# New prices in a planner of engine order, and a table that moves 312 groups of instructions, in a two-layer hybrid decoder

## The chip, the cores and the metric

The kernel runs on one core of a Trainium2 chip. The metric is the device time of one execution in microseconds (us). A core has five engines that run side by side, each through its own list of instructions: TensorE (PE in the profile; its weight loads are the row PEld), VectorE (DVE), ScalarE (ACT), GpSimd (POOL) and SyncE (SP), which here issues the loads and stores. They wait for each other by semaphores.

## The reference

The input is 1024 tokens of width 1024 in fp32, and there are two layers. A layer is a mixer and an FFN:

```python
for l in range(DEPTH):                          # 2
    h = rmsnorm(x, attn_norm[l])
    proj = h @ w_in[l]
    ...                                         # split into ten pieces
    y_a = mla_attention(...)                    # 4 heads, causal over all tokens, latent keys and values
    y_b = short_gated_conv(g_b, g_c, u_conv, conv_w[l])
    y_c = multiscale_pool(u_pool, pool_w[l], pool_scale[l])
    y_d = swa_sink_attention(...)               # 4 heads, window of 128 tokens
    ...                                         # each of the four normed over its 256 channels
    x = x + mixed @ w_o[l]
    h2 = rmsnorm(x, ffn_norm[l])
    gate, up = jnp.split(h2 @ w_gate_up[l], 2, axis=-1)
    x = x + (jax.nn.silu(gate) * up) @ w_down[l]
return rmsnorm(x, final_norm)
```

## The kernel before

**Layout and products.** Everything is held transposed: channels on the 128 partitions (rows), tokens along the free axis, in two halves of 512 tokens. fp32 products are made of three passes: an operand is split by ACT (the copy to `fp32r`, L281, L213 or L284) and by VectorE (what is left of it, L282, L214 or L285) into a high and a low part, and `mm3` (L270) multiplies high by high, high by low and low by high into one PSUM tile. PSUM tiles have four names with fixed buffers: `ps_mm` (2), `ps_s` (3), `ps_t` (2), `ps_pv` (1). Transposes (L479, L552, L942) and the sums over partitions for the norms (a product with a matrix of ones, L328) are true fp32; the rest of TensorE's work is `fp32r`.

**Stages.** Each layer goes through the input projection and the mixers, and then through the FFN, whose two matrix products are done with fewer block products (sums of weight blocks on GpSimd, L159, L1124 to L1126). In the mixer the steps that matter here are these. Sliding-window attention (`swa_unit`): scores L503, softmax, four transposes L552, split, products with the values L564, in 16 units per layer. Latent attention: values L270 into `ps_mm`, emptied by L820 and L821; for each of 4 heads and 2 halves, `scores` (L888 to L890), softmax, and `mix_values`: for each block of 128 keys transposes (L942) into a `ps_t` tile, the split into two tiles (L281, L282), and two products with the values (L954) into `ps_pv`. The output projection (L270 into `ps_mm`) is cut in parts and put between the heads. Its residual input is loaded at L1009, weights at L205, L210 and L257.

**What sets the order.** The program is first recorded in a written order. Then `order_engines` makes each engine's list anew. `steps_of` reads the instructions into steps (consecutive fp32 matmuls into one PSUM tile are one step) with their dependencies and a duration by kind. `arrange` plays the steps through a model of the five engines: at each point the engine that is free first takes, of its steps whose inputs are there and whose tiles have a free buffer, the one with the lowest rank, that is, the earliest in the written order. The sequence that comes out is fixed by dependencies between neighbours. The model's constants are matmul times (`MM_NS`), times between engines (`SIGNAL`), the overlap of neighbours on one engine (`OVERLAP`: VectorE's next instruction starts 82 ns before the end of the one before), and 92 ns on TensorE when an fp32 step follows an `fp32r` one. Nothing of this runs on the chip; only the lists do.

Of the kernel before, what the change touches and what calls it, by code (L numbers as in the profile page):

```python
# [1652 lines left out]
    "SP": {"PE": 50, "DVE": 35, "ACT": 35, "POOL": 80, "SP": 30},  # L1653
}
OVERLAP = {"DVE": 82, "ACT": 97, "POOL": 44}
FUNC_SETS = {"Silu": "Silu", "Exp": "Exp", "Ln": "Exp"}
ENGINES = {"PE": "PE", "DVE": "DVE", "Activation": "ACT", "Pool": "POOL", "SP": "SP"}


class Step:  # L1660
    __slots__ = ("ins", "eng", "rank", "before", "after", "tiles", "left", "ns", "tail", "ready", "sums", "bank", "onchip", "size", "start", "end", "table", "ls", "slotafter")

    def __init__(self, eng, rank):
        self.ins, self.eng, self.rank = [], eng, rank
        self.before, self.after, self.tiles = set(), [], set()
        self.ns = self.tail = self.ready = self.size = 0
        self.sums = self.bank = None
        self.onchip = False
        self.table = None


def areas(a):
# [25 lines left out]
DRAM_TILES = {"xs", "xp", "xr", "qd", "out"} | {f"ad{n}" for n in range(7)}  # L1698
# [34 lines left out]
def steps_of(tc):  # L1733
    steps, seen = [], {}
    table, runs = None, {"Silu": [], "Exp": []}
    for i in tc.nc.cur_bb.bb.instructions:
        kind = type(i).__name__
        if kind in ("BassTilePoolBoundary", "InstLoadActFuncSet"):
            continue
        eng = ENGINES[str(i.engine).split(".")[-1]]  # L1740
        ins = [a for a in i.ins if hasattr(a, "bass_ap")]
        outs = [a for a in i.outs if hasattr(a, "bass_ap")]
        fp32 = kind == "InstMatmult" and "float32r" not in str(i.ins[1].dtype)
        bank = outs[0].bass_ap.tensor.name
        v = steps[-1] if steps else None
        if not (fp32 and v and v.sums and v.bank == bank):
            v = Step(eng, len(steps))
            steps.append(v)
            v.bank, v.sums = bank, fp32
        v.ins.append(i)  # L1750
        if eng == "PE":
            n = width(outs[0])
            if fp32:
                one = i.ins[1].bass_ap.tensor.name.startswith("ones")
                v.ns += (867 if n == 512 else 534) if one else 108
                v.tail = 163 if one else 122
            else:
                v.ns = MM_NS[n]
                v.tail = 164 if n > 128 else 173
        elif kind == "InstDMACopy":  # L1760
            v.size = 4
            for s, n in outs[0].ap:
                v.size *= int(n)
            if eng == "POOL":
                v.ns, v.tail = 700, 4200
        else:
            v.ns = length(eng, kind, i, ins, outs)
            v.onchip = not any(a.bass_ap.tensor.name.startswith("ps_") for a in ins + outs)
            if eng == "ACT" and len(outs) > 1:
                v.tail = 61  # L1770
        f = FUNC_SETS.get(str(getattr(i, "func", "")).split(".")[-1])
        if f:
            other = runs["Exp" if f == "Silu" else "Silu"]
            if f != table:
                table = f
                runs[f] = []
            v.before |= set(other)
            runs[f].append(v)
            v.table = f
        for a, writes in [(a, False) for a in ins] + [(a, True) for a in outs]:  # L1780
            name, rects = areas(a)
            if kind == "InstCustomDveAnt":
                rects = [(0, 1 << 30, 0, 1 << 30)]
            if name.startswith("in_"):
                continue
            if name.split("_")[0] not in DRAM_TILES:
                v.tiles.add(name)
            seen.setdefault(name, [])
            for r, w, u in seen[name]:
                cross = name.startswith("ps_") and not (w or writes)  # L1790
                if cross or (w or writes) and any(
                    x[0] < y[1] and y[0] < x[1] and x[2] < y[3] and y[2] < x[3]
                    for x in r
                    for y in rects
                ):
                    v.before.add(u)
            seen[name].append((rects, writes, v))
    for v in steps:
        v.before.discard(v)
    return steps  # L1800


def arrange(steps, rank=lambda v: v.rank):
    queue, uses, freed, parked = {}, {}, {}, {}
    for v in steps:
# [3 lines left out]
        for name in v.tiles:  # L1809
            tag = name.rsplit("_", 1)[0]  # L1810
# [13 lines left out]
    now = {e: [] for e in SIGNAL}  # L1824
    out = {e: [] for e in SIGNAL}
    wire, pool_busy, last_fp32, table = 0.0, [], False, "Exp"
    for v in steps:
        if not v.left:
            heapq.heappush(later[v.eng], (0.0, rank(v), v.rank, v))
    while any(now.values()) or any(later.values()):  # L1830
        best = None
        for e in SIGNAL:
            if now[e]:
                t = free[e]
            elif later[e]:
                t = max(free[e], later[e][0][0])
            else:
                continue
            if best is None or t < best[0]:
                best = t, e  # L1840
        t, e = best
        while later[e] and later[e][0][0] <= t:
            _, k, n, v = heapq.heappop(later[e])
            heapq.heappush(now[e], (k, n, v))
        k, n, v = heapq.heappop(now[e])
        wait = None
        for name in v.tiles - live:
            tag = name.rsplit("_", 1)[0]
            if queue[tag][0] != name or not freed[tag]:
                parked[tag].append((k, n, v))  # L1850
                wait = -1
                break
            if freed[tag][0] + 40 > t:
                wait = max(wait or 0, freed[tag][0] + 40)
        if wait is not None:
            if wait > 0:
                heapq.heappush(later[e], (wait, k, n, v))
            continue
        for name in v.tiles - live:
            tag = name.rsplit("_", 1)[0]  # L1860
            live.add(name)
            queue[tag].popleft()
            heapq.heappop(freed[tag])
            for x in parked[tag]:
                heapq.heappush(later[x[2].eng], (t + 1, *x))
            parked[tag] = []
        v.start = t
        if v.size:
            if e == "SP":
                free[e] = t + 450  # L1870
                wire = max(t + 1400, wire) + v.size / 330.0
                v.end = wire + 600
            else:
                free[e] = t + v.ns
                v.end = t + v.ns + v.tail
        elif e == "PE":
            s = t + (92 if v.sums and not last_fp32 else 0)
            last_fp32 = v.sums
            free[e] = s + v.ns
            v.end = s + v.ns + v.tail  # L1880
        else:
            ns = v.ns
            if e == "DVE" and v.onchip:
                ns += 0.8 * sum(max(0.0, min(b, t + ns) - max(a, t)) for a, b in pool_busy[-8:])
            if v.table and v.table != table:
                table = v.table
                ns += 1280
            v.end = t + ns
            free[e] = v.end - OVERLAP[e]
            if e == "POOL":  # L1890
                pool_busy.append((t, v.end))
            if v.tail:
                free[e] = v.end - 10
                v.end += v.tail
        out[e].append(v)
        for name in v.tiles:
            todo[name] -= 1
            if not todo[name]:
                tag = name.rsplit("_", 1)[0]
                heapq.heappush(freed[tag], max(u.end for u in uses[name]))  # L1900
                for x in parked[tag]:
                    heapq.heappush(later[x[2].eng], (t + 1, *x))
                parked[tag] = []
        for w in v.after:
            x = free["PE"] if e == "PE" and w.eng == "PE" else v.end + SIGNAL["SP" if v.size else e][w.eng]
            if x > w.ready:
                w.ready = x
            w.left -= 1
            if not w.left:
                heapq.heappush(later[w.eng], (w.ready, rank(w), w.rank, w))  # L1910
    assert sum(map(len, out.values())) == len(steps)
    return out

def order_engines(tc):

    info = mybir.DependencyInfo(mybir.DependencyClass.NoSync, mybir.DependencyReason.DATA)
    for queue in arrange(steps_of(tc)).values():
        last = None
        for v in queue:
            for i in v.ins:  # L1920
# [131 lines left out]
```

## Time and profile before

| | us |
|---|---|
| median of 3 runs (lowest to highest) | 2083.02 (2080.73 to 2083.82) |
| profiled execution | 2081.12 |
| its span, first to last instruction | 2079.3 |
| TensorE busy | 2051.7 (99%) |
| VectorE busy | 1529.5 (74%) |
| ACT busy | 968.0 (47%) |
| GpSimd busy | 571.9 (28%) |

The span begins with the first layer's mixer (to about 416 us) and its FFN (to about 1092); the second layer's mixer runs to about 1456, its FFN to the end. How to read the rows that follow: in the rows by stretch, "a:b" is a stretch of the span, then its length, then the busy time and (instructions) of PE, PEld, DVE, ACT and POOL, the granted clock of TensorE as a share of full speed, the busy share of the DMA engines and GB/s. In rows in order of time, the first number is the start, the second the time from the first start to the last end of so many (x) instructions, and brackets hold the idle time of the engine before them with what ended it. In rows of the chain of work that ended last, the length of a piece is its share of that chain. A matmul is recorded from its start to the end of its results, while the next one starts earlier; so a busy TensorE need not be at its full pace.

### The profile page before, as it was taken

Reading aid. Unit: us, or ns where it says so; the run is one execution under the profiler, and the core shown is the slowest. Engines: PE = TensorE matmul, PEld = TensorE weight load, DVE = VectorE, ACT = ScalarE, POOL = GpSimd, SP = SyncE. Lnnn points to the kernel's source line nnn. Section 1 sums busy time; section 2 is a strip of 40 time slices with the busy share of each in tenths; the row PEclk is TensorE's granted clock in tenths of the full one; section 3 lists DMA queues with packets and bytes.
Section 4 is the critical chain, followed back from the end, with each engine's and each line's share of the span. In section 5 each row is a group of like instructions: output and inputs, shape, how many; then the busy total and the mean of one; then the engine's idle time right before and its main releaser. Section 6 shows DMA issues by size and latency. Waiting matters only on the chain.

```text
span 2079.3 us, 26320 instructions
## 1 busy us (share of the span) xinstructions
PE 2051.7 (99%) x9442; PEld 1679.6 (81%) x9442; DVE 1529.5 (74%) x2407; ACT 968.0 (47%) x1700; POOL 571.9 (28%) x453
## 2 busy tenths in 40 slices
PE   8999999999999999999999999999999999999997
PEld 6887777888888888888888877778888888888887
DVE  7878977977776777655657898869777677686555
ACT  6447656643333334444433566656433333354342
POOL 0000000037776775100000000000567677650000
PEclk9999999999999999999999999999999999999999
DMA  4110222424444446966401102232354444398652
GB/s 180 34 51 26 76 83 71 162 80 171 174 155 144 167 162 228 339 233 206 148 27 53 46 16 91 68 118 101 123 185 149 151 167 157 133 323 311 198 177 89
DMA packets 148819, 289.76 MB, mean 139 GB/s; under 512 B 12608, under 2 KB 72000, under 8 KB 148688
## 3 DMA queue, kind: packets, MB, share of 16 engines
q1 hardware_dynamic: 148656, 288.03, 40.1%
q8 instruction: 74, 1.21, 0.2%
q14 instruction: 57, 0.47, 0.1%
q0 software_dynamic: 32, 0.04, 0.0%
HBM read 204.66 MB, written 83.36 MB: 139 GB/s over the span
## 4 chain that ended last, share of the span: by engine, by line
PE 92%; DVE 6%; ACT 1%; DMA 1%; issue 0%; DVEq 0%; ACTq 0%; SPq 0%
PE ps_mm L270 34%; PE ps_s L270 29%; PE ps_t L270 12%; PE ps_pv L270 8%; PE ps_pv L954 2%; PE ps_t L942 1%; DVE u L282 1%; PE ps_s L888 1%; PE ps_pv L564 1%; PE ps_t L328 1%; PE ps_mm L762 1%; PE ps_s L503 1%; PE ps_s L890 1%; PE ps_s L889 1%; DVE u L340 1%; PE ps_t L552 1%
## 5 line engine op out<-in xcount | busy, mean ns | idle before, releaser
L270 PE MATMUL ps_mm<-u,u 128*128 128x512 f32 (+1 forms) x3376 | 825.8, 391 | 9.3 <-ACT u L284 7.1
L270 PEld LDWEIGHTS ps_mm<-u,u 128*128 128x128 f32 x3376 | 617.0, 189 | 131.6 <-ACT u L284 7.1
L270 PE MATMUL ps_s<-u,u 128*128 128x512 f32 x2672 | 630.7, 390 | 0.0
L270 PEld LDWEIGHTS ps_s<-u,u 128*128 128x128 f32 x2672 | 501.6, 188 | 106.3 <-issue 2.2
L282 DVE TENSOR_TENSOR u<-u,u 128x1024 fp32r<-128x1024 f32 (+2 forms) x368 | 443.4, 1230 | 148.7 <-ACT u L281 124.5
L281 ACT CAST u<-u 128x1024 fp32r<-128x1024 f32 (+2 forms) x368 | 321.1, 897 | 476.1 <-PE ps_mm L270 195.8
L270 PE MATMUL ps_t<-u,u 128*128 128x512 f32 (+1 forms) x1212 | 274.4, 379 | 0.0
L270 PEld LDWEIGHTS ps_t<-u,u 128*128 128x128 f32 x1212 | 219.1, 188 | 43.5 <-issue 1.4
L951 POOL MEMSET u<- 128x128 f32 x32 | 6.1, 217 | 865.8 <-PE ps_mm L270 628.8
L159 POOL TENSOR_TENSOR u<-u 128x256 f32<-128x256 f32 x176 | 188.4, 1071 | 68.9 <-DMA u<-in_w_dn 39.8
L1304 POOL TENSOR_TENSOR tp<-tp,u 128x512 f32<-128x512 f32 x88 | 144.0, 1638 | 223.2 <-ACT tp L1303 223.0
L270 PE MATMUL ps_pv<-u,u 128*128 128x512 f32 x696 | 164.9, 389 | 0.0
L270 PEld LDWEIGHTS ps_pv<-u,u 128*128 128x128 f32 x696 | 130.7, 188 | 27.1
L1303 ACT ACTIVATE tp<-tp 128x512 f32<-128x512 f32 x88 | 55.4, 632 | 119.6 <-DVE tp L340 118.6
L1124 POOL TENSOR_TENSOR u<-u,u 128x512 f32<-128x512 f32 x38 | 66.1, 1739 | 144.0 <-DMA u<-in_w_gu 81.9
L284 ACT ACTIVATE u<-u,par 128x512 fp32r<-128x512 f32 x100 | 69.9, 717 | 51.5 <-DVE u L1091 16.9
L282 DVE TENSOR_TENSOR u<-ps_t,u 128x512 fp32r<-128x512 f32 (+4 forms) x136 | 77.5, 584 | 21.7 <-ACT u L281 20.9
L281 ACT CAST u<-ps_t 128x512 fp32r<-128x512 f32 (+4 forms) x136 | 66.7, 505 | 57.0 <-PE ps_t L942 36.0
L285 DVE SCALAR_TENSOR_TENSOR u<-u,par,u 128x512 fp32r<-128x512 f32 x100 | 73.2, 751 | 8.3 <-ACT u L284 8.1
L1516 DVE TENSOR_TENSOR tp<-ps_mm,tn 128x512 f32<-128x512 f32 x38 | 26.3, 692 | 68.7 <-PE ps_mm L270 68.7
L214 DVE TENSOR_TENSOR u<-u,u 128x1024 fp32r<-128x1024 f32 (+1 forms) x46 | 51.8, 1129 | 33.2 <-ACT u L213 12.9
L1146 POOL TENSOR_TENSOR u<-u 128x512 f32<-128x512 f32 x38 | 68.3, 1797 | 8.9 <-DVE u L282 8.9
(186 smaller groups left out, 2240.2 us busy)
## 6 DMA issues: line engine op xcount, KB each, us to landing
u<-in_w_gu SPq DMA_DIRECT2D x88, 512.0 KB, 4.3
ad<-u SPq DMA_DIRECT2D x154, 256.0 KB, 2.5
u<-ad SPq DMA_DIRECT2D x70, 512.0 KB, 5.2
u<-in_w_dn SPq DMA_DIRECT2D x68, 512.0 KB, 3.9
qd<-u SPq DMA_DIRECT2D x44, 512.0 KB, 2.9
u<-qd SPq DMA_DIRECT2D x32, 512.0 KB, 4.7
u<-in_w_in SPq DMA_DIRECT2D x30, 512.0 KB, 3.5
u<-in_xT SPq DMA_DIRECT2D x32, 256.0 KB, 4.8
```

What stands on the lines that cost most here:

```text
L159: pool.tensor_tensor(out=o, in0=o, in1=u, op=ALU.add)
L214: dve.tensor_tensor(out=lo[:, :n], in0=raw[:, :n], in1=rd(hi[:, :n]), op=ALU.subtract)
L270: pe.matmul(o, w, r, start=start and k == 0 and i == 0, stop=stop and k == n - 1 and i == 2, skip_group_check=again,)
L281: act.copy(hi, f)
L282: dve.tensor_tensor(out=lo, in0=f, in1=rd(hi), op=ALU.subtract)
L284: act.activation(hi, f, AF.Copy, scale=gain)
L285: dve.scalar_tensor_tensor(out=lo, in0=f, scalar=gain, in1=rd(hi), op0=ALU.mult, op1=ALU.subtract)
L954: pe.matmul(py[:, c0:], v_of(j, h), R.ap(s)[:, c0:], start=j == 0 and n == 0, stop=j == nj - 1 and n == 1,)
L1124: pool.tensor_tensor(out=F.ap(q + 1), in0=a21, in1=a22, op=ALU.add)
L1146: pool.tensor_tensor(out=q4, in0=q4, in1=F.ap(self.raw[1] + 1), op=ALU.add)
L1303: last_silu = act.activation(g, g, AF.Silu)
L1304: pool.tensor_tensor(out=g, in0=g, in1=r, op=ALU.mult)
```

## The change

It touches the planner alone; what is computed stays. In `steps_of`, each step of an engine other than TensorE keeps the partition (row) at which its first input and its output start; two writes into one PSUM tile are now always ordered, as two reads were; the tiles of a step are a list in place of a set; and dependencies that follow from others are dropped. In `arrange`, VectorE and ACT start a step whose start rows differ from those of the one before only 31 and 24 ns after its end, in place of overlapping with it; after an fp32 step TensorE takes another ready fp32 step if there is one; a load of up to 128 KB is taken to land 1700 ns after its transfer in place of 600; steps parked for a buffer wake at a slightly later moment. And a table, `MOVES`, adds a number (from -300 to +164) to the rank of every step in 312 groups; a group is the steps of one engine on one output tile that stand near each other in the written order.

```diff
+SHIFT = {"DVE": 31, "ACT": 24, "POOL": 0}
...
+            if ins:
+                v.rows = tuple(areas(a)[1][0][0] for a in (ins[0], outs[0]))
...
-                cross = name.startswith("ps_") and not (w or writes)
+                cross = name.startswith("ps_") and w == writes
...
+    spare = [{u for w in v.before for u in w.before if u in v.before} for v in steps]
+    for v, far in zip(steps, spare):
+        v.before -= far
...
         k, n, v = heapq.heappop(now[e])
+        if e == "PE" and last_fp32 and not v.sums:
+            alike = [x for x in now[e] if x[2].sums and takes(x[2], t)]
+            if alike:
+                heapq.heappush(now[e], (k, n, v))
+                now[e].remove(min(alike))
+                k, n, v = min(alike)
+                heapq.heapify(now[e])
...
-                v.end = wire + 600
+                v.end = wire + (1700 if v.size <= 131072 else 600)
...
+            if v.rows:
+                rows, end = before[e]
+                if rows != v.rows and (rows[1] or v.rows[0]):
+                    t = max(t, end + SHIFT[e])
...
+MOVES = {
+    2: -39, 5: -32, 10: -33, 30: 2, 35: 5, 40: -8, 51: -20, 52: -31, 55: 88, 62: -146, 100: -12,
...
+    4598: 75,
+}
+
+
+def places(steps):
+
+    groups, last, at = {}, {}, {}
+    for v in steps:
+        k = v.bank, v.eng
+        if k not in groups or v.rank - last[k] > 60:
+            groups[k] = len(at)
+            at[groups[k]] = None
+        last[k] = v.rank
+        v.place = v.rank + MOVES.get(groups[k], 0)
+    return steps
...
-    for queue in arrange(steps_of(tc)).values():
+    for queue in arrange(places(steps_of(tc)), lambda v: v.place).values():
```

More of the change, by code (lines that the diff above doesn't have):

```diff
@@ L1660 @@
 class Step:
-    __slots__ = ("ins", "eng", "rank", "before", "after", "tiles", "left", "ns", "tail", "ready", "sums", "bank", "onchip", "size", "start", "end", "table", "ls", "slotafter")
+    __slots__ = ("ins", "eng", "rank", "before", "after", "tiles", "left", "ns", "tail", "ready", "sums", "bank", "onchip", "size", "start", "end", "table", "rows", "place")
     def __init__(self, eng, rank):
         self.ins, self.eng, self.rank = [], eng, rank
-        self.before, self.after, self.tiles = set(), [], set()
+        self.before, self.after, self.tiles = set(), [], []
         self.ns = self.tail = self.ready = self.size = 0
@@ L1668, in __init__ @@
         self.onchip = False
-        self.table = None
+        self.table = self.rows = None
 def areas(a):
@@ L1785, in steps_of @@
                 continue
-            if name.split("_")[0] not in DRAM_TILES:
-                v.tiles.add(name)
+            if name.split("_")[0] not in DRAM_TILES and name not in v.tiles:
+                v.tiles.append(name)
             seen.setdefault(name, [])
             for r, w, u in seen[name]:
-                cross = name.startswith("ps_") and not (w or writes)
+                cross = name.startswith("ps_") and w == writes
                 if cross or (w or writes) and any(
@@ L1826, in arrange @@
     wire, pool_busy, last_fp32, table = 0.0, [], False, "Exp"
+    before = {e: ((0, 0), 0.0) for e in SHIFT}
     for v in steps:
@@ L1829, in arrange, with takes @@
             heapq.heappush(later[v.eng], (0.0, rank(v), v.rank, v))
+    def takes(v, t):
+        for name in (x for x in v.tiles if x not in live):
+            tag = name.rsplit("_", 1)[0]
+            if queue[tag][0] != name or not freed[tag] or freed[tag][0] + 40 > t:
+                return False
+        return True
     while any(now.values()) or any(later.values()):
@@ L1845, in arrange @@
         k, n, v = heapq.heappop(now[e])
+        if e == "PE" and last_fp32 and not v.sums:
[5 more added lines that the diff above has]
+                heapq.heapify(now[e])
         wait = None
-        for name in v.tiles - live:
+        for name in (x for x in v.tiles if x not in live):
             tag = name.rsplit("_", 1)[0]
@@ L1858, in arrange @@
             continue
-        for name in v.tiles - live:
+        for name in [x for x in v.tiles if x not in live]:
             tag = name.rsplit("_", 1)[0]
@@ L1894, in arrange @@
                 v.end += v.tail
+            if v.rows:
+                before[e] = v.rows, v.end
         out[e].append(v)
@@ L1901, in arrange @@
                 for x in parked[tag]:
-                    heapq.heappush(later[x[2].eng], (t + 1, *x))
+                    heapq.heappush(later[x[2].eng], (v.start + 1, *x))
                 parked[tag] = []
```

34 rows, old and new, of the table MOVES are left out of this document.

## The prediction

> **What bounds the kernel now.** I read the page's first part, then the busy time by stretches, then the chain and the instructions in order of time at the places where TensorE loses time.
>
> ```profile
> span 2079.3 us, 26320 instructions
> PE 2051.7 (99%) x9442; PEld 1679.6 (81%) x9442; DVE 1529.5 (74%) x2407; ACT 968.0 (47%) x1700; POOL 571.9 (28%) x453
> ...
> 52.00:416.00 364.00, 359.68 (x1736) 286.94 (x1735) 308.20 (x700) 216.33 (x482) 3.02 (x16) 1.00 0.21 72
> 416.00:1092.00 676.00, 676.00 (x2994) 558.73 (x2993) 458.42 (x519) 267.72 (x379) 284.51 (x208) 1.00 0.50 172
> 1092.00:1456.00 364.00, 359.69 (x1719) 287.86 (x1718) 303.49 (x669) 213.27 (x462) 3.11 (x16) 1.00 0.21 70
> 1456.00:2028.00 572.00, 572.00 (x2523) 473.39 (x2523) 395.18 (x407) 222.82 (x299) 280.40 (x208) 1.00 0.54 189
> ```
>
> TensorE is the bound, and in the two FFN stretches (416 to 1092, 1456 to 2028) it is so without a gap. 572.00 us for 2523 matmuls are 226.7 ns each, the pace at which 512-wide products follow each other in the longest unbroken piece of the chain (22.44 us for 99):
>
> ```profile
> 828.22 22.44 PE ps_s L270 x99
> ...
> 2043.68 7.92 PE ps_mm L270 x66
> ...
> L270 PE MATMUL ps_s<-u,u 128*128 128x512 f32 x2672 | 630.7, 390 | 0.0
> L942 PE MATMUL ps_t<-cst,u 128*128 128x128 f32 x288 | 45.0, 275 | 1.0 <-DVE u L282 1.0
> L328 PE MATMUL ps_t<-u,ones 128*128 128x512 f32 x52 | 27.3, 613 | 0.8 <-DVE u L318 0.4
> ...
> 7.11 3.35 PE L270 MATMUL ps_mm<-u,u 128*128 128x512 f32 x6 [7.11 <-ACT u L284]
> ...
> 2069.35 0.70 PE L328 MATMUL ps_s<-u,ones 128*128 128x256 f32 x2 [1.48 <-DVE u L318]
> ```
>
> "99% busy" hides time lost in the other stretches, because a 512-wide product is recorded as 390 ns while the next starts after 227. So I count products instead, in the built program: 8148 of 512 columns (1846.9 us at 226.7 ns), 704 of 256 (84.5 at 120 ns, from 7.92/66), 80 of 384 (13.9, halfway between), 16 narrow ones (1), 424 transposes (45.8 at 108 ns, measured below), and 35 products with the ones, two passes of 613 - 163 = 450 ns (31.4; 163 is the overlap 390 - 227). Together 2023.5 us. From the first start, 7.11, to the last end, 2070.05 less that overlap, pass 2062.8. TensorE thus loses 39 us between its first and last product, 1.5 of it in the last wait (1.48 in the row); next to nothing of it is in the FFN, so some 37 lie in the start and the two mixer stretches (0 to 416, 1092 to 1456). Only 4.3 us in each of the two long mixer rows show as idle (364.00 less 359.68, less 359.69).
>
> The Trainium skill (Perfetto Trace Analysis, "Identifying the Most-Contended Engine") says that matmul busy time misleads, and to look at the weight loads' share. The trace agrees: 78.8% and 79.1% in the two mixer rows, against 82.7% and 82.8% in the FFN rows, under an equal 99 to 100% of matmul. By that measure the 574.8 us of loads in both mixer rows would need 695 us at the FFN's share, where they take 728: an estimate of 33 us lost, beside the 37 that my count gives with the start.
>
> **What the order of instructions shows.** In the built program the FFN stretches are the same instruction by instruction on TensorE; only the two mixers, their loads, and the last 30 us are reordered. So at most the 37 us and the last 1.5 us are at stake. The tail after the last product (2070.05 to 2079.3) keeps its chain; only its last stores swap places, all of one size: nothing.
>
> **Part 1, the gap at a change of partitions.**
>
> ```profile
> 58.36 0.69 DVE L428 TENSOR_TENSOR u<-te,u 64x512 fp32r<-64x512 f32 x1
> 59.08 0.69 DVE L431 TENSOR_TENSOR u<-te,u 64x512 fp32r<-64x512 f32 x1
> 59.80 0.69 DVE L340 TENSOR_TENSOR u<-ps_mm,u 128x512 f32<-128x512 f32 x1
> 60.41 0.35 DVE L513 CUSTOM_DVE_ANT_0 ps_s<-ps_s,cst,nsink 128x128 f32<-128x128 f32 x1
> ```
>
> L431 and L340 start 0.03 us after the end before them, L513 0.08 us before it: a change of the rows costs 0.11 us on VectorE. The program has 130 such changes before and 131 after: knowing them removes none. The direct worth is 0 (one more is 0.1 us on an engine that is 74% busy); the list merely stops planning on results that come 0.1 us later. The Trainium skill (VectorE: DVE Perf Modes, "Two Vector instructions with no wait between them") states it as hardware: an instruction whose operands start in another quadrant of partitions than those before it is held until all earlier ones have finished. The rows agree, and it speaks against any gain from this part alone: see the first rival.
>
> **Part 2, transposes taken together.** A new rule lets TensorE, after an fp32 step, take another ready fp32 step first. Changes from fp32r into fp32 fall from 147 to 110. Price, from this stretch of layer 1:
>
> ```profile
> 338.82 0.60 PE L942 MATMUL ps_t<-cst,u 128*128 128x128 f32 x4
> 339.17 0.48 PE L888 MATMUL ps_s<-u,u 128*128 128x512 f32 x1
> 339.49 0.39 PE L889 MATMUL ps_s<-u,u 128*128 128x512 f32 x1
> 339.72 0.40 PE L890 MATMUL ps_s<-u,u 128*128 128x512 f32 x1
> 339.95 0.60 PE L942 MATMUL ps_t<-cst,u 128*128 128x128 f32 x4
> 341.17 0.50 PE L954 MATMUL ps_pv<-u 128*128 128x512 f32 x1 [0.61 <-ACT u L281]
> 342.14 0.63 PE L942 MATMUL ps_t<-cst,u 128*128 128x128 f32 x4 [0.47 <-DVE u L282]
> 342.52 0.71 PE L954 MATMUL ps_pv<-u,u 128*128 128x512 f32 x2
> 343.12 0.66 PE L942 MATMUL ps_t<-cst,u 128*128 128x128 f32 x4
> 343.54 0.72 PE L954 MATMUL ps_pv<-u,u 128*128 128x512 f32 x2
> 344.49 5.27 PE L270 MATMUL ps_mm<-u,u 128*128 128x512 f32 x20 [0.24 <-ACT u L213]
> ```
>
> Four transposes last 0.60, the last of them 0.275 (its row's mean): 108 ns each. From 338.82 to 339.72 are 0.90 us for four of them (0.43) and two products (0.45): the change costs about 0.015. The kernel's own list prices it at 92 ns. So 37 changes are worth 0.5 us (3.4 by the list's constant). I take 0.5.
>
> **Part 3, the moved groups: three kinds of waits.**
> (a) The last head of a layer. From 339.95 to 344.49 TensorE does twelve transposes (1.30) and five products (1.13) in 4.54 us: 2.1 lost, since a transposed block needs ACT's copy and DVE's subtraction, 0.9 us from the last transpose (339.95 + 0.32) to the first product (341.17), and nothing else stands between. In the new order two blocks are transposed in a row, 0.85 us of scores follow, then four products together, later another pair of blocks with output-projection products between. Layer 2 adds a late weight:
>
> ```profile
> 1367.97 0.47 PE L954 MATMUL ps_pv<-u,u 128*128 128x512 f32 x1
> 1369.34 0.80 PE L270 MATMUL ps_mm<-u,u 128*128 128x512 f32 x2 [0.89 <-ACT u L213]
> ...
> 1362.81 5.57 DMA u<-in_w_o
> ```
>
> There the projection that waited 1.14 us (1.37 less one product) starts earlier in the new order. Of 2.1 and, for the like place with this, some 2.6 I take 3 as regained.
> (b) The value products.
>
> ```profile
> 233.49 0.40 PE L890 MATMUL ps_s<-u,u 128*128 128x512 f32 x1
> 235.09 0.70 PE L270 MATMUL ps_mm<-u,vhi 128*128 128x512 f32 x2 [1.21 <-DVE u L821]
> ```
>
> 1.60 less 0.23 is 1.37 lost until VectorE has emptied the bank. Between the last product into that bank and the next stand 1.5 us of work now, 2.4 in the new order, in both layers. Twice 0.85: 1.7.
> (c) All short covers. For each of the 96 split blocks of L942 I add up the TensorE work between its last transpose and its first product; under 1.2 us are 49 before, 34 after; of the 60 blocks of L552, 27 and 14. Together 76 and 48, 37% fewer; the medians go from 1.17 to 1.61 us and from 1.72 to 2.11. Of the 37 us, 4.7 + 2.7 are in (a) and (b), 2 in changes: 30 are left, of which I take a fifth, 6, as regained. The bounds are below nothing (the moves have opened new short covers, -2) and the full 37%, 11.
>
> Sum: 0 + 0.5 + 3 + 1.7 + 6 = 11.2, with the small start-up fillers some 12. The profiled execution took 2081.1 (span 2079.3 and 1.8 around it); the median of the runs is 2083.0. From it: 2071.
>
> **The rivals.**
> Full already, or not what it says: TensorE is 99% busy, the gaps stay (130 and 131) and the moves only shuffle. For it the page's row and the unchanged count; against it the 39 us counted and the longer covers. 2083. A twin, where the list's clock is off and the plan falls apart on the chip, gives 1 to 4 us: 2079 to 2082.
> Slower, by the load queue. SyncE issues all loads in one row, and a load that stands earlier but waits for its place holds those behind it:
>
> ```profile
> SPq L205 <- PE ps_pv L564: 67.0, 6, 35.0
> ```
>
> The longest such wait is 35.0 us already. The new order moves weight and residual loads in both mixers. If a weight tile then lands late by one load (5.57 us in the row above), TensorE loses up to 4; it takes four such tiles to eat the 12 us and pass the mark: 2087 to 2091. Against it: the idle times of TensorE quoted above name work of ACT or DVE; only the 0.89 goes back to a load.
> Larger: the places are so well chosen that two thirds of the 37 us go: 2059 to 2063.
>
> **How the numbers follow.** Forecast, 2064 to 2077: 0.62. Larger gain, below 2064: 0.12. A small gain, 2077 to 2082: 0.13, most of it beyond 0.2% (4.2 us, about what a measurement of this kernel can tell from no change). Full already: 0.07. Slower: 0.06. So faster 0.84, within 0.2% 0.10, slower 0.06. The range 2060 to 2080 reaches into the larger and the small gain and leaves out about 2 in 10.
>
> **What would show it.** TensorE's busy time near 2042 with the same 9442 instructions; weight-load share of the mixer stretches above 80%; the waits of 0.61, 0.47 and 1.21 us gone or halved; the FFN stretches at 226.7 ns. A mixer stretch as long as before, or waits of TensorE for loads, would prove it wrong.

## The result and the profile after

The changed kernel takes 2068.16 us (median of 4 runs, 2066.81 to 2069.08); the kernel before, in the runs beside it, 2082.47 (4 runs, 2080.73 to 2083.82). The ratio is 0.9931, 95% interval [0.9914, 0.9948]: 14.3 us faster. From one profiled execution to the other, 2081.12 to 2069.08, it is 12.0. The forecast was 2071 in a range of 2060 to 2080.

The first part of the page of the changed kernel, and its busy time by stretches (columns as before: length, then PE, PEld, DVE, ACT, POOL, clock, DMA share, GB/s):

```profile
span 2067.3 us, 26298 instructions
PE 2043.4 (99%) x9442; PEld 1681.0 (81%) x9442; DVE 1533.3 (74%) x2407; ACT 966.2 (47%) x1700; POOL 568.9 (28%) x453
```
```profile
52.00:416.00 364.00, 362.35 (x1763) 294.14 (x1762) 311.85 (x704) 217.69 (x483) 2.83 (x16) 1.00 0.21 72
416.00:1092.00 676.00, 674.20 (x2983) 556.40 (x2981) 451.21 (x511) 266.61 (x377) 280.79 (x208) 1.00 0.50 173
1092.00:1456.00 364.00, 362.08 (x1749) 293.83 (x1748) 308.83 (x673) 217.30 (x467) 6.60 (x19) 1.00 0.21 72
1456.00:2028.00 572.00, 571.54 (x2537) 473.18 (x2536) 400.28 (x412) 220.21 (x300) 277.75 (x206) 1.00 0.54 187
```

The same 9442 matmuls now take 2043.4 us of TensorE. In both mixer rows the share of weight loads rose, from 78.8% and 79.1% to 80.8% and 80.7%: more products got through in the same 364 us. But the first FFN row, full before (676.00 of 676.00), now has 1.8 us of idle time and a smaller weight-load share, 82.3% instead of 82.7%. The windows stand still while the work moves forward through them, so I also count the loss directly. **Loss** below is, summed over a stretch, the time from the start of one TensorE instruction to the start of the next, less the pace of its kind (226.7 ns for a 512-wide product, 108 for a transpose, and so on as in the prediction).

| loss, us | mixers and start (0 to 416, 1092 to 1456) | FFNs | all, with the last wait |
|---|---|---|---|
| before | 38.7 | 0.7 | 40.9 |
| after | 23.4 | 3.9 | 28.9 |

So the mixers gave 15.3 us, and the FFNs took 3.2 back. The two sites that the prediction named, in the order of time of the changed kernel's TensorE:

```profile
228.47 0.39 PE L890 MATMUL ps_s<-u,u 128*128 128x512 f32 x1
229.12 0.36 PE L270 MATMUL ps_mm<-vhi,u 128*128 128x256 f32 x1 [0.27 <-DVE u L821]
...
335.85 1.03 PE L942 MATMUL ps_t<-cst,u 128*128 128x128 f32 x8
337.46 0.73 PE L270 MATMUL ps_mm<-u,u 128*128 128x512 f32 x2 [0.57 <-ACT u L213]
338.03 0.39 PE L954 MATMUL ps_pv<-u 128*128 128x512 f32 x1
...
1252.32 0.40 PE L890 MATMUL ps_s<-u,u 128*128 128x512 f32 x1
1252.91 0.70 PE L270 MATMUL ps_mm<-u,vhi 128*128 128x512 f32 x2 [0.19 <-DVE u L821]
...
1356.07 1.03 PE L942 MATMUL ps_t<-cst,u 128*128 128x128 f32 x8
1358.49 3.85 PE L270 MATMUL ps_mm<-u,u 128*128 128x512 f32 x15 [1.39 <-ACT u L213]
```

The value products, which waited 1.21 us for VectorE, wait 0.27 and 0.19. At the last head of layer 1 eight transposes now run in one piece, and the idle time of 0.61 and 0.47 us for ACT and VectorE is gone. In its place stands a wait for ACT's copy of a weight (L213). Such waits are not new, only longer: before, those for L213 at the last heads were 0.24 us in layer 1 and 0.89 in layer 2. The chain shows what that copy waited for:

```profile
330.72 5.84 DMA u<-in_w_o
336.57 0.84 ACT u L213
...
1351.52 0.19 PE ps_pv L954
1351.71 0.02 SPq L205
...
1351.76 5.77 DMA u<-in_w_o
```

A weight of the output projection arrives late in both layers, 5.84 and 5.77 us after its issue. That is the late weight tile of the prediction's "slower" rival, at 0.57 and 1.39 us instead of up to 4. That another load held it back, as the rival has it, does not show here: in layer 2 its issue (L205) follows the end of a product (L954).

### The profile page after: what moved, and what is told of

Its sections match the earlier page's. It is cut to its first block, busy times and chain, and to the rows that moved or that the text cites. A ratio compares the mean times of both kernels' runs of the same rounds, so it can differ in the third digit from the quotient of the medians.

```text
span 2067.3 us, 26298 instructions
## 1 busy us (share of the span) xinstructions
PE 2043.4 (99%) x9442; PEld 1681.0 (81%) x9442; DVE 1533.3 (74%) x2407; ACT 966.2 (47%) x1700; POOL 568.9 (28%) x453
## 3 DMA queue, kind: packets, MB, share of 16 engines
q8 instruction: 74, 1.21, 0.2%
## 4 chain that ended last, share of the span: by engine, by line
PE 95%; DVE 2%; DMA 1%; ACT 1%; POOL 1%; issue 1%; DVEq 0%; SPq 0%; ACTq 0%
PE ps_mm L270 36%; PE ps_s L270 29%; PE ps_t L270 12%; PE ps_pv L270 7%; PE ps_pv L954 2%; PE ps_t L942 1%; PE ps_t L328 1%; PE ps_s L888 1%; PE ps_pv L564 1%; PE ps_s L890 1%; PE ps_s L889 1%; PE ps_s L503 1%; PE ps_t L552 1%; DMA u<-in_w_o 1%; PE ps_mm L762 1%
## 5 line engine op out<-in xcount | busy, mean ns | idle before, releaser
L270 PE MATMUL ps_mm<-u,u 128*128 128x512 f32 (+1 forms) x3376 | 836.8, 390 | 9.1 <-ACT u L284 7.1
L270 PE MATMUL ps_s<-u,u 128*128 128x512 f32 x2672 | 639.0, 390 | 0.7 <-ACT tn L1168 0.7
L270 PE MATMUL ps_t<-u,u 128*128 128x512 f32 (+1 forms) x1212 | 292.1, 380 | 0.0
L159 POOL TENSOR_TENSOR u<-u 128x256 f32<-128x256 f32 x176 | 188.1, 1069 | 69.9 <-DVE u L282 31.8
L270 PE MATMUL ps_pv<-u,u 128*128 128x512 f32 x696 | 170.6, 389 | 1.5 <-ACT tn L1168 1.1
L1303 ACT ACTIVATE tp<-tp 128x512 f32<-128x512 f32 x88 | 55.2, 632 | 121.4 <-DVE tp L340 120.6
L340 DVE TENSOR_TENSOR tp<-tp,u 128x512 f32<-128x512 f32 x76 | 67.6, 889 | 1.1
L316 ACT ACTIVATE tn<-u 128x512 f32<-128x512 f32 (+1 forms) x93 | 52.9, 589 | 32.8 <-DVE u L1569 28.3
```

The costliest lines, as they stand in the source:

```text
L159: pool.tensor_tensor(out=o, in0=o, in1=u, op=ALU.add)
L270: pe.matmul(o, w, r, start=start and k == 0 and i == 0, stop=stop and k == n - 1 and i == 2, skip_group_check=again,)
L316: act.activation(q, f, AF.Square)
L340: dve.tensor_tensor(out=o, in0=a, in1=b, op=ALU.mult)
L1303: last_silu = act.activation(g, g, AF.Silu)
```

## Experiments

The theories: (A) the moved places bring the gain and the rules are nearly free; (B) the rules, by telling the planner the truth, bring it; (C) neither does much alone, since the table was made for this planner. Unless a diff says otherwise, each kernel is the changed kernel with the one edit shown, so the small edits to how steps are read (ordered writes, the list of tiles, the later wake) stay in all of them. The kernel before, on the same chips, ran at 2082.49 us (first four kernels: the two halves, first_layer_moves, pool_kept), 2081.32 (the next four) and 2081.22 (the last three).

### The two halves: rules_alone and table_alone

```diff
-        v.place = v.rank + MOVES.get(groups[k], 0)
+        v.place = v.rank
```

> The table is emptied; the new prices and rules of the planner stay. Changes into fp32 on TensorE: 128 (147 before, 110 with the table). Theory A (the moved places bring the gain): 2078 to 2082 us, a gain of 1 to 4, and most waits in both mixers stay. Theory B (the list's better clock brings it, since it no longer plans on results that come late): 2070 to 2074 us.

```diff
-        if e == "PE" and last_fp32 and not v.sums:
+        if False and e == "PE" and last_fp32 and not v.sums:
...
-                v.end = wire + (1700 if v.size <= 131072 else 600)
+                v.end = wire + 600
...
-                if rows != v.rows and (rows[1] or v.rows[0]):
+                if False and rows != v.rows and (rows[1] or v.rows[0]):
```

> The table stays; the gap at a change of rows, the rule of taking fp32 steps together and the 1700 ns for small loads are taken back. Changes into fp32: 126. Theory A: 2069 to 2075 us. Theory B: 2078 us or more, since the places were chosen for another clock. A third, that the two need each other: both this and the rules alone gain under 5 us, and the sum falls short of the 14 of both.

The rules alone take 2077.50 us (ratio 0.9975 [0.9965, 0.9985]), the table alone 2078.76 (0.9982 [0.9973, 0.9992]): 5.0 and 3.7 us, 8.7 if they added, where both together give 14.3. So C, though neither half is idle: some 4 to 6 us come only where table and rules meet. It is 5.6 between the medians, with intervals of some 2 us or more on each term, and 4.0 by the loss of the mixers in the profiles (38.7 before, 32.9 and 33.2 with one half, 23.4 with both). The table's own entries in the FFNs show too: with the rules alone the FFNs lose 0.9 us, with the table alone 4.0.

### One layer's moves: first_layer_moves

```diff
-        v.place = v.rank + MOVES.get(groups[k], 0)
+        v.place = v.rank + (MOVES.get(groups[k], 0) if groups[k] < 2000 else 0)
```

> Only the table's entries up to group 1279 (the first layer) stay, with all rules. If the gains are local and add up: the first mixer is as short as in the changed kernel, the second as with the rules alone, and the time lies about halfway, 2073 to 2076. If a layer's order hangs on the other's: outside of that.

2073.10 us (0.9952 [0.9937, 0.9967]). The loss of layer 1's mixer with the start is 13.6 us, as in the changed kernel (13.4); layer 2's is 15.5, near that of the rules alone (14.1), where the changed kernel has 10.0; a stretch of halved clock, told of below under part 3 (c), is 1.7 of the 15.5. The moves work where they stand; one layer's do not need the other's.

### The FFN waits: pool_kept, no_ffn_moves, pool_price

In the changed kernel TensorE takes the products of the FFN in another order and stands still there. First its order of time before, where a tile gets its 24 products in one piece:

```profile
460.84 5.60 PE L270 MATMUL ps_t<-u,u 128*128 128x512 f32 x24
```

Then the changed kernel, its order of time, ACT's and the waits:

```profile
463.44 0.39 PE L270 MATMUL ps_t<-u,u 128*128 128x512 f32 x1
463.66 0.39 PE L270 MATMUL ps_s<-u,u 128*128 128x512 f32 x1
...
467.94 3.04 PE L270 MATMUL ps_s<-u,u 128*128 128x512 f32 x12 [0.72 <-ACT tn L1168]
...
503.14 2.88 PE L270 MATMUL ps_pv<-u,u 128*128 128x512 f32 x12
505.86 2.88 PE L270 MATMUL ps_mm<-u,u 128*128 128x512 f32 x12
509.82 3.01 PE L270 MATMUL ps_pv<-u,u 128*128 128x512 f32 x12 [1.08 <-ACT tn L1168]
512.68 0.61 PE L270 MATMUL ps_mm<-u,u 128*128 128x512 f32 x2
```
```profile
507.72 0.63 ACT L1303 ACTIVATE tp<-tp 128x512 f32<-128x512 f32 x1 [6.51 <-DVE tp L340]
508.26 1.03 ACT L281 CAST u<-u 128x1024 fp32r<-128x1024 f32 x1
509.19 0.58 ACT L1168 COPY tn<-ps_pv 128x512 f32<-128x512 f32 x1
```
```profile
PE ps_pv L270 <- ACT tn L1168: 1.1, 1, 1.1
PE ps_s L270 <- ACT tn L1168: 0.7, 1, 0.7
```

The twelve products of 503.14 fill the one `ps_pv` buffer. ACT should empty it at 506.02, but its copy (L1168) stands in ACT's list behind L1303, which waits 6.51 us for a VectorE result, and behind a cast. ACT is busy 39% of that row and still late: an in-order list holds a ready copy behind one that is not ready. TensorE is held the same way. The Trainium skill (TensorE: Matmul & The Clock Gate, "The mechanism") says that matmuls start and end strictly in their order. The trace is in line with it: the `ps_mm` products of 512.68 came behind the ones that waited 1.08 us; whether they were ready sooner, it does not show.

First suspect was GpSimd, whose FFN list had changed too. pool_kept chains its instructions in the order of before; TensorE's list stays that of the changed kernel:

```diff
+    for row in POOL_ROWS:
+        for a, b in zip(row, row[1:]):
+            steps[b].before.add(steps[a])
```

> The changed kernel, with GpSimd's list in both FFN stretches held in the order that it had before (TensorE's list is the same as in the changed kernel). If the new waits of TensorE in the FFN (1.1, 0.7 and 0.5 us for ACT's copies) come from GpSimd's swapped steps: they go, and the time falls by 2 to 3.5 us, to 2065 to 2066. If they come from the earlier arrival at the FFN with loads or stores not further on: they stay, 2068.

2069.71 us (0.9939 [0.9924, 0.9954]): no help, and the waits for L1168 stay, 1.9 and 1.6 us. The second suspect was the six entries of the table that fall in the FFNs, all on TensorE: `ps_t` and `ps_s` products of layer 1, `ps_mm`, `ps_s`, `ps_t` and `ps_s` of layer 2, 12 to 48 products each.

```diff
-    1106: -110, 1111: -40, 1112: -44, 1116: -37, 1140: -41, 1146: 57, 1263: -6, 1279: -31, 2267:
+    1106: -110, 1111: -40, 1112: -44, 1116: -37, 1140: -41, 1146: 57,   2267:
...
-    163, 3463: -25, 3581: 22, 3586: 22, 3620: -51, 4570: 95, 4583: 119, 4589: 83, 4595: 134,
+    163,     4570: 95, 4583: 119, 4589: 83, 4595: 134,
```

> The changed kernel without the table's six entries that lie in the FFN (groups 1263, 1279, 3463, 3581, 3586 and 3620); both mixers keep all moves. If these six make the new waits of TensorE in the FFN (2.8 us in layer 1, 1.0 in layer 2 of the changed kernel): the waits go, 2064 to 2066 us. If the waits come from something else (an earlier arrival, GpSimd's chain): 2067 to 2069, with the waits in place.

2064.57 us (4 runs, 2064.22 to 2064.94; 0.9921 [0.9906, 0.9936]), faster than the changed kernel by 3.6 between medians, and by 2.4 if each is set against the kernel before beside it (16.8 gained, and 14.3). TensorE's order differs from the changed kernel's only where the six entries stand, in stretches of 117, 36 and 149 instructions. The time by stretches and the same place in the order of time:

```profile
416.00:1092.00 676.00, 676.00 (x3001) 559.08 (x2999) 456.40 (x514) 267.13 (x378) 282.06 (x208) 1.00 0.50 173
...
1456.00:2028.00 572.00, 572.00 (x2559) 474.83 (x2558) 395.06 (x415) 220.89 (x301) 267.95 (x202) 1.00 0.54 187
```
```profile
502.27 2.88 PE L270 MATMUL ps_pv<-u,u 128*128 128x512 f32 x12
504.99 2.88 PE L270 MATMUL ps_mm<-u,u 128*128 128x512 f32 x12
507.71 2.88 PE L270 MATMUL ps_pv<-u,u 128*128 128x512 f32 x12
```

Both FFNs are full again, their loss falls from 3.9 to 0.5 us, and no wait for L1168 is left. Here ACT's L1303 starts at 504.65, in time. The six entries were the cause. pool_price asks instead whether the planner's low price of a 256-wide GpSimd addition is to blame (760 ns, where the trace of after has 1069 for L159):

```diff
-        return 206 if kind == "InstMemset" else 230 + 2.07 * n
+        return 206 if kind == "InstMemset" else 1150 if n == 256 else 230 + 2.07 * n
```

> The changed kernel, with GpSimd's 256-wide sums priced at 1150 ns in the planner, as the profile has them (1071 ns mean), and not at 760. TensorE's list is the same as in the changed kernel. If the new FFN waits come from plans that hold GpSimd free too early: they shrink, 2064 to 2067 us. If they come from TensorE's own order: 2067 to 2069.

2067.22 us (2066.57 to 2068.31; 0.9934 [0.9919, 0.9949]). Its runs overlap those of the changed kernel, so no gain is shown; TensorE's list is the same. Measured beside no_ffn_moves, it is the fair partner for the six entries: 2.7 us, with no overlap of the runs.

### The rules beside the table: no_grouping, no_gaps, price_15

```diff
-        if e == "PE" and last_fp32 and not v.sums:
+        if False and e == "PE" and last_fp32 and not v.sums:
```

> The changed kernel without the rule that takes ready fp32 steps together. Changes into fp32: 121 in place of 110. By the price of 15 ns that the trace of before gives: 0.2 us for the changes themselves. If only the changes count: 2068 to 2069 us. If the rule is part of the plan that the table was made for (the moves need the same rules): 2070 to 2075, with longer waits at other places. By the list's 92 ns the changes alone would be 1.0 us.

```diff
-                if rows != v.rows and (rows[1] or v.rows[0]):
+                if False and rows != v.rows and (rows[1] or v.rows[0]):
```

> The changed kernel without the gap at a change of rows in the planner; the table stays. The prediction gave this part a direct worth of 0. If it only serves the plan, as the need of table and rules for each other says: 2071 to 2077 us, since 130 starts on VectorE come 0.11 us later than planned and the moves were made for the right times. If it is worth nothing: 2067 to 2069.

2075.33 us (0.9972 [0.9961, 0.9982]) and 2076.37 (0.9978 [0.9968, 0.9987]): leaving out either rule costs 7.2 and 8.2 us between medians, and 8.3 and 9.4 if each is set against the kernel before beside it, though the first changes the number of changes into fp32 by only 11 (121 for 110), 0.2 us at 18 ns each. One can explain that in two ways: the rule is right and the plan needs a true clock, or any other planner spoils the table. The third kernel helps to tell these apart. It makes one price *truer*:

```diff
-            s = t + (92 if v.sums and not last_fp32 else 0)
+            s = t + (15 if v.sums and not last_fp32 else 0)
```

> The changed kernel with the planner's price of a change into fp32 at 15 ns in place of 92, the size that both traces show; 114 changes in place of 110, 49 short covers in place of 48. If a truer clock makes a better list: 2068 or less. If the table holds only for the planner as it stands, wrong price included: slower, 2070 to 2076.

2075.46 us (7 runs, 2074.84 to 2076.56; 0.9971 [0.996, 0.9983]): 7.3 slower than the changed kernel (8.6 if each is set against the kernel before beside it). A truer price costs as much as a missing rule. Waits of TensorE that are not among the changed kernel's stand in the profile of each (no_gaps, no_grouping, price_15, in this order):

```profile
PE ps_mm L270 <- DVE te L340: 1.4, 1, 1.4
PE ps_s L888 <- ACT u L281: 1.1, 1, 1.1
PE ps_s L888 <- ACT u L907: 1.0, 1, 1.0
```
```profile
PE ps_s L888 <- ACT u L281: 1.1, 1, 1.1
...
PE ps_s L888 <- ACT u L907: 1.0, 1, 1.0
```
```profile
PE ps_s L888 <- ACT u L281: 2.2, 2, 1.1
PE ps_mm L270 <- DVE te L340: 1.9, 2, 1.6
...
PE ps_s L888 <- ACT u L907: 1.4, 2, 1.0
```

The first scores of the attention (L888) wait for ACT in all three. So what a rule is worth beside this table is not the time that it describes: with any of the three changed, the list is no longer the one for which the places fit. That the truer price costs time because of the table, and would not without it, was not run.

### The places themselves: shifted_moves

```diff
+NEXT = dict(zip(MOVES, [*MOVES.values()][1:] + [*MOVES.values()][:1]))
...
-        v.place = v.rank + MOVES.get(groups[k], 0)
+        v.place = v.rank + NEXT.get(groups[k], 0)
```

> The changed kernel with each number of the table given to the next group of the table: the same 312 groups and the same numbers, at wrong places; rules as in the changed kernel. If the particular places are what the rules need: no better than the rules alone, 2077 or more, and the counts say so (131 changes into fp32, 57 of 196 blocks with short cover, where the changed kernel has 110 and 48). If any spreading of the order does it: about 2068.

2096.82 us (1.0073 [1.0059, 1.0087]): 15.6 slower than before, where the rules without any table gained 5.0. The time by stretches, and what TensorE waited for:

```profile
52.00:416.00 364.00, 355.87 (x1724) 285.53 (x1723) 301.06 (x690) 212.60 (x473) 2.88 (x16) 1.00 0.21 72
...
1092.00:1456.00 364.00, 356.84 (x1726) 286.91 (x1725) 302.97 (x689) 213.60 (x473) 3.25 (x16) 1.00 0.21 71
1456.00:2028.00 572.00, 567.92 (x2488) 466.72 (x2487) 387.39 (x405) 218.24 (x296) 275.80 (x208) 1.00 0.54 185
```
```profile
PE ps_pv L270 <- ACT tn L1168: 2.3, 2, 1.9
PE ps_mm L270 <- DVE te L340: 1.9, 2, 1.1
PE ps_s L270 <- ACT tn L1168: 1.9, 2, 1.4
PE ps_mm L270 <- DVE u L821: 1.9, 1, 1.9
PE ps_s L888 <- ACT u L907: 1.8, 3, 1.2
```

The mixers lose 43.0 us and the FFNs 11.9, of which 4.2 are waits for L1168 as above. The numbers belong to their groups; this one shift of them is not neutral but harmful.

### The best version: best_both

The edits of no_ffn_moves and pool_price together.

> The changed kernel without the six moves of FFN groups, and with the planner's price of a 256-wide GpSimd step at 1150 ns in place of 760; TensorE's list is that of no_ffn_moves to the instruction, only VectorE, ACT and GpSimd are reordered in the FFNs. If what the price saved in pool_price (1 us) came from the waits that the six moves made, nothing is left to save: 2064 to 2065.5. If GpSimd's true price is worth something of its own in an FFN without waits: 2063 to 2064.

2064.43 us (5 runs, 2063.80 to 2065.16; 0.9918 [0.9904, 0.9932]): the fastest together with no_ffn_moves, from which it can't be told apart. The GpSimd price shows no worth once the FFN waits are gone. One difference shows that something is left: layer 2's late weight. The lines give the time from issue to landing of such loads, no_ffn_moves first (with another load in its window, so that the last number counts), best_both second:

```profile
DMA to landing us min/median/max: 2.9/3.5/4.2
```
```profile
DMA to landing us min/median/max: 5.5/5.5/5.5
```

In no_ffn_moves it landed in 4.2 us and TensorE did not wait; in best_both it took 5.5, and TensorE waited 1.15. The lists of TensorE are the same, those of SyncE, ACT and VectorE are not. The issue is no later: in both it stands 4.3 us ahead of the same eight transposes, with the same loads next to it in SyncE's list. What makes the load take longer was not tried.

## Why the prediction was right, and where it was not

**The bound and the count: right.** TensorE's lost time, not its busy share, was the thing to read: the count of 39 us (40.9 when counted step by step) became 28.9, and that difference, 12.0, is the whole difference of the two profiled executions.

**"The FFN stretches are the same instruction by instruction on TensorE": wrong.** Six entries of the table reorder the beginning of each FFN, in stretches of up to 149 instructions. The loss there rose by 3.2 us, and dropping the entries gained 2.4 to 3.6. The prediction gave this term 0, and would have been off by it had others not been too small.

**Part 1, the gaps, and part 2, transposes together: prices right, meaning incomplete.** Changes into fp32 fell to 110 and cost, there and back, a median of some 15 to 20 ns in both traces, beside the 15 forecast and the planner's 92: about 0.7 us. The gaps stayed on the chip. But "the direct worth is 0" says nothing of the plan: without either rule the table loses 7 to 9 us.

**Part 3 (a): mechanism right, a little less.** The eight transposes at 335.85 take 0.87, so 0.7 us are lost there for 2.1 before; in layer 2 it is 1.6 for 2.6. That is 2.4 for 3, since the late weight took the rest: the wait for it in layer 2, which the prediction had among the 2.6, did not shrink but grew, from 0.89 to 1.39.

**Part 3 (b): right.** 229.12 less 228.47 less 0.23 is 0.42 us and the like of layer 2 (1252.91 less 1252.32) 0.36, for 1.37 before in layer 1 and 1.36 in layer 2: 2.0 regained for 1.7.

**Part 3 (c): too small, by a measure that does not hold.** Of the 15.3 us of the mixers, 2.4, 2.0 and 0.7 are named; 10.2 remain. Of these 1.7 are neither covers nor waits but the clock. In the profile of before, right behind the waits of layer 2's last head, products follow each other in 0.43 us instead of 0.227, and the granted clock is 0.62 of full speed over 4.5 us, where it is 1.00 at the like place of the changed kernel (1356 to 1362):

```profile
1369.00:1373.50 4.50, 4.17 (x13) 3.38 (x14) 4.13 (x5) 2.40 (x4) 0.35 (x2) 0.62 0.20 83
```

The missing 0.38 of 4.5 us is 1.7 us. The prediction named no such term; the profiles of first_layer_moves (mixer of layer 2) and shifted_moves (FFN of layer 2) have one like it. What sets it off is not shown. That leaves 8.5 us for (c) and the start, where 6 and 0.8 were taken, and the bound of (c) was 11. The fifth was a choice under the 37% by which the short covers fell, and the experiments show that their number does not rank the kernels:

| kernel | short covers (of 96 + 60) | mixers' loss, us |
|---|---|---|
| before | 76 | 38.7 |
| rules_alone | 62 | 32.9 |
| shifted_moves | 57 | 43.0 |
| table_alone | 56 | 33.2 |
| no_gaps | 51 | 31.0 |
| price_15 | 49 | 29.9 |
| after | 48 | 23.4 |

Between price_15 and after it is one cover and 6.5 us; shifted_moves has 19 fewer than before and loses more. (The expectation for that run counts 196 blocks; those of the prediction are 156.) Waits that the covers do not count (scores for ACT, banks for L340 and L821) stand in their place in the profiles above. So it was in part luck that the forecast of 12 met the profiled difference of 12.0: a term too small by 1.7 and a clock that cost 1.7 before and was not counted met a loss of 3.2 in the FFNs that was taken as nothing. The rest of the 14.3 between medians is within the spread of the runs.

**The rivals.** "Full already" fell by the trace. "Slower, by the load queue" was there as a late weight, at 2.0 us of waits for L213 in place of 1.1. "Where the list's clock is off and the plan falls apart", a gain of 1 to 4 us, is what table_alone does, with its old prices: 3.7. The shifted table goes further: at wrong places a table costs 15.6 us. The forecast's own caution, "waits of TensorE for loads would prove it wrong", was too strong: two of them came, the one of layer 2 at a load that was waited for before too, and were small.

What stays open: how the 1700 ns for small loads and the edits to how steps are read share in the gain (they were left in or taken out only together with others), why the truer price of a change costs time, what makes the late weight take 4.2 or 5.8 us, and why the table misses the FFN on the chip.

## What to carry to other kernels

A table of places fits the planner that reads it: a truer constant or a missing rule cost 7 to 9 us here, and shifted entries 29 to 30. So change the planner first and make the table anew after it (which was not tried here), and test entries by stretches, dropping those where the engine was already full. Judge an order by start-to-start loss on the engine that bounds, stretch by stretch; a proxy such as the count of short covers can improve while the time gets worse. Where an engine at 40% busy appears as the releaser, look in its list for what stands ahead of the instruction that was waited for.

## What the runs showed of the hardware that was not expected

A change from fp32r to fp32 on TensorE and back costs some 15 to 20 ns (median of all changes in both traces), a fifth of what the planner charges. The time from issue to landing of one and the same weight load varied from 4.2 us (no_ffn_moves) to 5.8 (after) between kernels whose TensorE orders and issues do not differ there, which alone makes or takes away a wait of 1.2 to 1.4 us. And the granted clock can fall to 0.62 over 4.5 us in the midst of a kernel whose mean clock is 0.998, at 1.7 us: easily missed, and more than any one wait that the change removes.
